# RWKV chunk: both heads' inverse products as one product, the outputs of a unit at its end

## The chip, the core and the metric

One core of a Trainium2 chip runs the kernel in one launch. The metric is the device time of one execution in microseconds, as the median of several runs. The engines are named as in the profile: PE is TensorE's matmul, PEld its weight load, DVE is VectorE, ACT is ScalarE, POOL is GpSimd and SP is SyncE, which issues the DMAs.

## The reference

One layer of a decoder for 1024 prompt tokens and 8 sample tokens. It projects the normalised input, runs an RWKV-7 recurrence (8 heads of 64) beside a diagonal state-space branch, merges the two through gates, and ends with a convolutional feed-forward net, a per-layer embedding and a norm. The change lies in the recurrence, which is, for one head:

```
sa  = S @ (-kk_t)
S   = S * w_t + sa (kk_t * a_t)^T + v_t k_t^T
y_t = S @ r_t
```

The results are all outputs y, the last states and the projected rows, in fp32.

## The kernel before

All arithmetic of TensorE is fp32 or a pair of float32r parts. A float32 product is issued by the program once and stands in the trace as two passes, each with its own weight load.

**Stream.** Most of the time goes to large projections (tile psm, `mtile` and `mt`): weights come by DMA (wraw), are split in two float32r parts (whi on ACT, wlo on POOL or DVE), and three products per 128x128 weight tile go into one of three PSUM banks (pool pm). In the stretch of interest these are the last gate tiles (344 columns, inputs h1h, h1l), then the GLU of the state-space branch (zh, zl), then the first half of the merge and feed-forward part for 512 tokens (mid, act).

**Units.** The recurrence is worked in 8 units (`build_rwkv`, line 1626 on): a unit is a pair of heads p (two heads of 64 lie on the 128 partitions) and a half hf of the prompt, 512 tokens, that is NC = 8 chunks of CH = 64 tokens. `prepare` makes a unit's inputs (`stage_a`, elementwise; `stage_g`, the products within chunks and the inverse of their triangular part), `chain` walks the 8 chunks, and `post` norms the outputs and sends them to DRAM. `prepare(n + 1)` is recorded ahead of `chain(n)`.

**Within chunks.** `stage_g` (line 1424) multiplies BK and AR of each chunk and head, masks the 128x128 result into Gm (DVE, four chunks at once), and transposes BK into BT. Gm holds for each chunk and head 128 columns: 64 for the inverse (A part) and 64 for the outputs (r part). The lower half of the A columns is replaced by its product with v (tile gvp, ACT). The inverse of the unit triangular 64x64 blocks is made in 32x32 blocks: two DMAs through DRAM, 31 steps on DVE (Tm), two DMAs back, and 2 x 16 products of 32x32 (mgp). Gm, BT and UV have two buffers, so the preparation of a unit can write them when the chain two units earlier has ended.

**Chain.** For chunk c (line 1520 on), with the state S of both heads as a block diagonal 128x128 tile: (1) pp = AR^T S, one 128x128 product; (2) DVE adds Gm's upper A rows into pe; (3) up, the inverse product: for each head a product with 64 output rows, Gm's 64 A columns as weights and 64 columns of pe moving, both into partitions 0 to 63 of up; (4) the outputs of the chunk before (`inner`): for each head, UV as weights and Gm's 64 r columns moving, into partitions 64h to 64h + 63 of the bank Y; (5) DVE copies up into UV; (6) su = BT^T UV, a 128x128 product; (7) Y += S^T r, a 128x128 product against 64 columns; (8) for each head DVE makes the new S from su and the decayed old one (sw, ACT). pp, up and su are three 128-column parts of one PSUM bank (tile chp); Y fills another bank (tile Yps), of which there is one. The products of (3) and (4) have the shape 128x64 in the profile, all others of the chain 128x128. The first chunk of a unit has no `inner`; the outputs of its last chunk stand after the loop.

**Order.** No engine's order is written out by hand: `Sched` records each operation with its dependencies, an estimated cost and a priority, and issues the operations engine by engine in the order of modelled time (`run`, line 354, `issue`, line 378; every issued instruction therefore stands on line 417). A lower number goes first: weight loads and the emptying of the stream's banks have HI, units have SIDE + 100000 n + 20000 k (k = 0 preparation, 1 chain, 2 post), the stream has MAIN. So a stream product is taken when no operation of a unit is ready by the planner's clock. A change of TensorE's shape is planned at 90 ns (SWITCH). `then` adds a dependency for the plan alone, so that a product isn't taken before some other operation.

Of the kernel before, what the change touches and what calls it, by code (L numbers as in the profile page):

```python
# [9 lines left out]
F32 = mybir.dt.float32  # L10
F32R = mybir.dt.float32r
AF = mybir.ActivationFunctionType
# [3 lines left out]
MUL, ADD, SUB, MAX, MIN = ALU.mult, ALU.add, ALU.subtract, ALU.max, ALU.min  # L16

P = 128
# [9 lines left out]
CH = 64  # L28
HW = 512
NC = HW // CH  # L30
# [1257 lines left out]
def build_rwkv(g, rp, pb, pch, py, I, O, Pd, Wd, Ad, Yd, sg, ssh, omu, pc, pcs, dscr, dap, dma,  # L1288
               epst, rsqrt):
    V, S, G, T, _ = g.engines()  # L1290
# [9 lines left out]
    mask4 = cc("mask")[:, None, :].to_broadcast([P, 4, 128])  # L1300
# [40 lines left out]
    for k in range(2):  # L1341
        t = rp.tile([P, P], F32, name=f"pe{k}")
# [80 lines left out]

    def stage_g(p, hf, a):
        AR, BK, v = a["AR"], a["BK"], a["v"]
        Gm = rp.tile([P, NC, 2, P], F32, name="Gm", tag="Gm", bufs=2)
        BT = rp.tile([P, NC, P], F32, name="BT", tag="BT", bufs=2)
        UV = rp.tile([P, NC, P], F32, name="UV", tag="UV", bufs=2)
        fl = lambda z: z.rearrange("p a b -> p (a b)")
        free = [G.memset(z, 0.0) for z in (Gm[:, 0, 0, 0:1], BT[:, 0, 0:1], UV[64:128, 0, 0:1])]  # L1430
        mm = lambda i, *a: g.rec("PE", "matmul", T.ns.matmul, a, dict(start=True, stop=True),
                                 (free[i],))
        tr = lambda i, *a: g.rec("PE", "transpose", T.ns.transpose, a, {}, (free[i],))
        for c4 in range(0, NC, 4):
            gp = [big(f"gp{h}").rearrange("p (c t) -> p c t", t=P) for h in range(2)]
            for j in range(4):
                for h in range(2):
                    hs = slice(64 * h, 64 * h + 64)
                    mm(0, gp[h][:, j], fl(BK[hs, c4 + j]), fl(AR[hs, c4 + j]))
            for h in range(2):  # L1440
                V.tensor_tensor(Gm[:, c4:c4 + 4, h], gp[h], mask4, op=MUL)
            tp = big("tpp").rearrange("p (c t) -> p c t", t=P)
            for j in range(4):
                tr(1, tp[:, j], fl(BK[:, c4 + j]), ident)
            S.activation(BT[:, c4:c4 + 4], tp, AF.Copy)
            vp = big("vpp").rearrange("p (c t) -> p c t", t=P)
            for c in range(c4, c4 + 4):
                if c == 0:
                    mm(2, vp[64:128, 0], v[:, 0:CH], ident)
                else:  # L1450
                    tr(2, vp[:, c - c4], v[:, (c - 1) * CH:(c + 1) * CH], ident)
            S.activation(UV[64:128, c4:c4 + 4], vp[64:128], AF.Copy)

        for c4 in range(0, NC, 4):
            vp = big("gvp")[64:128].rearrange("p (c h t) -> p c h t", h=2, t=64)
            for c in range(c4, c4 + 4):
                for h in range(2):
                    T.matmul(vp[:, c - c4, h], Gm[64:128, c, h, 0:64],
                             UV[64:128, c, 64 * h:64 * h + 64], start=True, stop=True)
            S.activation(Gm[64:128, c4:c4 + 4, :, 0:64], vp, AF.Copy)  # L1460


        gs = Gm.rearrange("p a b t -> p (a b) t")
        dg = [gs[32 * k:32 * k + 32, :, 32 * k:32 * k + 32] for k in range(2)]
        ld = dscr_ring("ld")
        for k in range(2):
            dma(dap(ld, 16384 * k, [[32, 32], [1024, 2 * NC], [1, 32]]), dg[k])
        Tm = rp.tile([P, 8, 32], F32, name="Tm", tag="Tm", bufs=2)
        tmp = rp.tile([P, 8, 32], F32, name="Tt", tag="Tq", bufs=2)
        dma(Tm, I["con"][:, nc_:nc_ + 256].rearrange("p (a b) -> p a b", b=32))  # L1470
        L = rp.tile([P, 31, 32], F32, name="Lj", tag="Lj", bufs=1)
        for r in range(4):
            dma(L[32 * r:32 * r + 32], dap(ld, 0, [[1024, 32], [1, 31 * 32]]))
        for j in range(31):
            n, w = j // 4 + 1, 31 - j
            if n == 1:
                V.scalar_tensor_tensor(Tm[:, 0, j + 1:], L[:, j, j + 1:], Tm[:, 0, j:j + 1],
                                       Tm[:, 0, j + 1:], op0=MUL, op1=ADD)
                continue
            V.tensor_tensor(tmp[:, :n, :w], L[:, None, j, j + 1:].to_broadcast([P, n, w]),  # L1480
                            Tm[:, :n, j:j + 1].to_broadcast([P, n, w]), op=MUL)
            V.tensor_tensor(Tm[:, :n, j + 1:], Tm[:, :n, j + 1:], tmp[:, :n, :w], op=ADD)
        xd = dscr_ring("xd")
        dma(dap(xd, 0, [[32, P], [4096, 8], [1, 32]]), Tm)
        for k in range(2):
            dma(dg[k], dap(xd, 512 * k, [[1024, 32], [32, 2 * NC], [1, 32]]))

        av = rp.tile([64, 2 * NC, 32], F32, name="av", tag="av", bufs=1)
        V.transpose(av[0:32], dg[0])
        mp = big("mgp").rearrange("p (a t) -> p a t", t=32)  # L1490
        for j in range(2 * NC):
            T.matmul(mp[32:64, j], gs[0:32, j, 32:64], av[0:32, j], start=True, stop=True)
        S.activation(av[32:64], mp[32:64], AF.Copy)
        mp = big("mgp").rearrange("p (a t) -> p a t", t=32)
        for j in range(2 * NC):
            T.matmul(mp[0:32, j], av[32:64, j], gs[32:64, j, 32:64], start=True, stop=True)
        S.activation(gs[0:32, :, 32:64], mp[0:32], AF.Copy)
        return dict(Gm=Gm, BT=BT, UV=UV)
# [7 lines left out]
    def chain(p, hf, a, b):  # L1506
        AR, WC, Gm, BT, UV = a["AR"], a["WC"], b["Gm"], b["BT"], b["UV"]
        Y = py.tile([P, NC, CH], F32, name="Yps", tag="Y")
        ch = pch.tile([P, 3, P], F32, name="chp", tag="ch")
        pp, up, su = ch[:, 0], ch[0:64, 1], ch[:, 2]  # L1510
        heads = [slice(64 * h, 64 * h + 64) for h in range(2)]

        def then(op, *a, **k):
            g.rec("PE", "matmul", T.ns.matmul, a, k, (op,))

        def inner(c, op, first):
            for h, hs in enumerate(heads):
                then(op, Y[hs, c], UV[:, c, hs], Gm[:, c, h, 64:128], start=first, stop=True)

        for c in range(NC):  # L1520
            n = hf * NC + c
            So, Sn = St[p, n % 2], St[p, (n + 1) % 2]
            first = n == 0

            if not first:
                T.matmul(pp, AR[:, c].rearrange("p a b -> p (a b)"), So, start=True, stop=True)
            pe = rhs[n % 2]
            gv = Gm[64:128, c, :, 0:64]  # L1530
            if first:
                got = V.tensor_copy(pe[0:64].rearrange("p (h t) -> p h t", t=64), gv)
            else:
                h2 = lambda z: z.rearrange("p (h t) -> p h t", t=64)
                got = V.tensor_tensor(h2(pe[0:64]), h2(pp[0:64]), gv, op=ADD)
            for h, hs in enumerate(heads):
                T.matmul(up[:, hs], Gm[:, c, h, 0:64], pe[:, hs], start=h == 0, stop=h == 1)
            if c:
                inner(c - 1, got, n == 1)
            got = V.tensor_copy(UV[0:64, c], up)  # L1540
            sw = rp.tile([P, P], F32, name="sw", tag="sw", bufs=2)
            for hs in heads:
                if not first:
                    S.activation(sw[hs, hs], So[hs, hs], AF.Copy, scale=WC[hs, c:c + 1])
            T.matmul(su, BT[:, c], UV[:, c], start=True, stop=True)
            if not first:
                then(got, Y[:, c], So, AR[:, c, 1], start=True, stop=False)
            for hs in heads:
                if first:
                    done = V.tensor_scalar(Sn[hs, hs], su[hs, hs], WC[hs, c:c + 1], None, op0=MUL)  # L1550
                else:
                    done = V.scalar_tensor_tensor(Sn[hs, hs], su[hs, hs], WC[hs, c:c + 1],
                                                  sw[hs, hs], op0=MUL, op1=ADD)
            if n == 2 * NC - 1:
                for hs in heads:
                    dma(O["wkv_p"][p][hs], Sn[hs, hs])
        inner(NC - 1, done, False)
        Y = Y.rearrange("p c t -> p (c t)")
        hi = rp.tile([P, HW], F32R, name="yh", tag="ysq", bufs=1)
        lo = claimed("yl", F32R)  # L1560
        S.activation(hi, Y, AF.Copy)
        V.tensor_tensor(lo, Y, hi.bitcast(F32), op=SUB)
        return hi, lo
# [204 lines left out]
```

## Time and profile before

| | us |
|---|---|
| median of 3 runs | 1861.35 |
| lowest, highest | 1857.27, 1863.98 |
| the profiled execution | 1858.5 |
| its span | 1856.7 |
| first to last inverse product (chp<-pe) | 335.4 to 827.2 |

The page gives each engine's busy time in the span. In the timeline of TensorE a row has its start, its length, the tile written and those read, the shape of the weights and of the moving data, and how many passes it merges. Lengths of matmuls are modelled and overlap, so the distance between two starts is the time that TensorE gave to the first. The clock that the throttle granted is a share of full speed.

### The profile page before, as it was taken

How to read it: one execution, taken by the hardware profiler on the slowest of the kernel's cores; microseconds unless marked ns; L12 is line 12 of the kernel's file. 1: busy time of each engine (PE TensorE's matmuls, PEld its weight loads, DVE VectorE, ACT ScalarE, POOL GpSimd, SP SyncE). 2: the span in 40 equal slices, each digit the busy share in tenths (PEclk: the TensorE clock that was granted, in tenths of full speed). 3: DMA queues.
4: the chain of work that ended last, by engine and by line, in shares of the span. 5: the costliest groups of instructions: out<-in, count | busy, mean ns of one | idle time of the engine just before them, and what ended most of it. 6: DMA issues, size and time to landing. Idle time of an engine off the chain costs nothing.

```text
span 1856.7 us, 32382 instructions
## 1 busy us (share of the span) xinstructions
PE 1799.0 (97%) x11946; PEld 1616.2 (87%) x11946; DVE 1135.5 (61%) x2376; ACT 810.6 (44%) x1445; POOL 738.7 (40%) x1071
## 2 busy tenths in 40 slices
PE   7999999999999999999999999999999999999997
PEld 6988888888889988987788888888888999999997
DVE  8899357758776568767655334335646445445475
ACT  4242443355544555554533333334655333323364
POOL 0000022233332444236654545455656444444464
PEclk9998998989999999999999999999999999999999
DMA  5534864313322264345633323223233333233332
GB/s 199 160 112 151 261 212 121 102 55 97 114 72 82 92 192 133 106 145 173 215 127 114 97 91 94 92 93 103 91 99 98 106 92 95 89 92 98 87 94 89
DMA packets 157949, 219.80 MB, mean 118 GB/s; under 512 B 48208, under 2 KB 81488, under 8 KB 157648
## 3 DMA queue, kind: packets, MB, share of 16 engines
q1 hardware_dynamic: 157792, 217.74, 37.7%
q8 instruction: 94, 1.54, 0.4%
q14 instruction: 63, 0.52, 0.1%
HBM read 174.94 MB, written 42.92 MB: 117 GB/s over the span
## 4 chain that ended last, share of the span: by engine, by line
PE 71%; DVE 10%; DMA 4%; ACT 3%; issue 3%; POOL 2%; SPq 1%; POOLq 0%; DVEq 0%; ACTq 0%
PE psm L417 62%; PE chp L417 2%; PE gp L417 1%; DMA yf<-yq 1%; DVE Tm L417 1%; PE gvp L417 1%; DVE Tt L417 1%; PE Yps L417 1%; DMA raw<-pd 1%; SPq L417 1%; DVE m L417 1%; DVE cv L417 1%; POOL wlo L417 1%; DMA wraw<-in_w_rw_out 1%; DVE Xi L417 1%
## 5 line engine op out<-in xcount | busy, mean ns | idle before, releaser
L417 POOL TENSOR_TENSOR wlo<-wraw,whi 128x512 fp32r<-128x512 f32 (+2 forms) x432 | 546.3, 1271 | 455.1 <-ACT whi L417 424.1
L417 PE MATMUL psm<-act,whi 128*128 128x260 f32 (+1 forms) x2880 | 651.9, 320 | 2.2 <-ACT whi L417 1.6
L417 PEld LDWEIGHTS psm<-act,whi 128*128 128x128 f32 x2880 | 479.8, 188 | 49.3 <-ACT whi L417 2.6
L417 ACT ACTIVATE whi<-wraw 128x512 fp32r<-128x512 f32 (+2 forms) x468 | 276.9, 597 | 447.9 <-PE psm L417 280.0
L417 PE MATMUL psm<-act,wlo 128*128 128x260 f32 (+1 forms) x1440 | 459.5, 322 | 0.0
L417 PE MATMUL psm<-mid,whi 128*128 128x260 f32 (+1 forms) x1344 | 306.1, 321 | 3.3 <-DVE cv L417 2.3
L417 PEld LDWEIGHTS psm<-act,wlo 128*128 128x128 f32 x1440 | 270.2, 188 | 23.5 <-issue 0.5
L417 PE MATMUL psm<-h1h,whi 128*128 128x344 f32 x816 | 271.0, 333 | 11.6 <-DVE h1h L417 11.3
L417 PE MATMUL psm<-h1h,wlo 128*128 128x344 f32 x816 | 270.7, 332 | 0.3 <-DVE wlo L417 0.2
L417 PE MATMUL psm<-h1l,whi 128*128 128x344 f32 x816 | 270.7, 332 | 0.1
L417 PEld LDWEIGHTS psm<-mid,whi 128*128 128x128 f32 x1344 | 222.7, 189 | 21.9 <-DVE cv L417 2.5
L417 PE MATMUL psm<-mid,wlo 128*128 128x260 f32 (+1 forms) x672 | 213.7, 322 | 0.0
L417 PEld LDWEIGHTS psm<-h1h,whi 128*128 128x128 f32 x816 | 156.7, 192 | 15.2 <-ACT h1h L417 11.3
L417 DVE TENSOR_TENSOR x<-psm,x 128x260 f32<-128x260 f32 (+1 forms) x160 | 84.6, 532 | 132.7 <-PE psm L417 132.6
L417 PEld LDWEIGHTS psm<-h1l,whi 128*128 128x128 f32 x816 | 157.0, 192 | 3.6 <-issue 0.9
L417 PEld LDWEIGHTS psm<-h1h,wlo 128*128 128x128 f32 x816 | 156.7, 192 | 3.7 <-DVE wlo L417 0.9
L417 PEld LDWEIGHTS psm<-mid,wlo 128*128 128x128 f32 x672 | 126.5, 189 | 9.6 <-POOL wlo L417 0.6
L417 DVE TENSOR_TENSOR ta<-psm,rs 128x260 f32<-128x260 f32 (+1 forms) x66 | 34.0, 516 | 139.0 <-PE psm L417 132.1
L417 DVE SCALAR_TENSOR_TENSOR cv<-ta,par,cv 128x512 f32<-128x512 f32 x88 | 89.7, 1019 | 38.3 <-ACT cv L417 36.9
L417 DVE TENSOR_TENSOR mid<-cv,mid 128x260 fp32r<-128x260 f32 (+1 forms) x84 | 67.3, 808 | 34.0 <-ACT mid L417 33.9
L417 ACT ACTIVATE sw<-S,WC 64x64 f32<-64x64 f32 x120 | 41.4, 345 | 74.5 <-DVE S L417 69.7
L417 ACT ACTIVATE cv<-cv 128x512 f32<-128x512 f32 (+1 forms) x44 | 28.0, 636 | 87.6 <-DVE cv L417 87.6
(348 smaller groups left out, 2557.3 us busy)
## 6 DMA issues: line engine op xcount, KB each, us to landing
wraw<-in_w_ffn_in SPq DMA_DIRECT2D x176, 256.0 KB, 2.7
wraw<-in_w_in SPq DMA_DIRECT2D x68, 256.0 KB, 3.4
wraw<-in_w_ffn_out SPq DMA_DIRECT2D x64, 192.0 KB, 2.4
gd<-gt SPq DMA_DIRECT2D x16, 516.0 KB, 3.2
wraw<-in_w_out SPq DMA_DIRECT2D x32, 256.0 KB, 2.9
wraw<-in_w_ple_gate SPq DMA_DIRECT2D x32, 256.0 KB, 2.7
wraw<-in_w_ffn_out SPq DMA_DIRECT2D x32, 256.0 KB, 3.2
pd<-pt SPq DMA_DIRECT2D x12, 516.0 KB, 3.8
```

What stands on the lines that cost most here:

```text
L417: o.fn(*o.args, **o.kw)
```

## The change

`Gm` gets its A and r parts as the outer of its column dimensions, so that the 64 A columns of both heads of a chunk lie side by side as 128. The inverse product becomes one 128x128 product against all 128 columns of pe; its result has both heads' blocks on the diagonal (partitions 0 to 63 with columns 0 to 63, partitions 64 to 127 with columns 64 to 127) and two cross blocks that nobody reads. DVE copies the two diagonal blocks in two instructions, the second from partitions 64 to 127 to partitions 0 to 63. `inner` is gone from the loop: after the last chunk, 16 products (8 chunks, 2 heads) add the outputs to Y, planned after the last state update. Only the first product into Y starts the bank; all others add or write where nothing stands yet.

```diff
@@ stage_g
-        Gm = rp.tile([P, NC, 2, P], F32, name="Gm", tag="Gm", bufs=2)
+        Gm = rp.tile([P, 2, NC, 2, CH], F32, name="Gm", tag="Gm", bufs=2)
+        halves = lambda z: z.rearrange("p c (k t) -> p k c t", t=CH)
...
-                V.tensor_tensor(Gm[:, c4:c4 + 4, h], gp[h], mask4, op=MUL)
+                V.tensor_tensor(Gm[:, :, c4:c4 + 4, h], halves(gp[h]), halves(mask4), op=MUL)
...
-                    T.matmul(vp[:, c - c4, h], Gm[64:128, c, h, 0:64],
+                    T.matmul(vp[:, c - c4, h], Gm[64:128, 0, c, h],
...
-            S.activation(Gm[64:128, c4:c4 + 4, :, 0:64], vp, AF.Copy)
+            S.activation(Gm[64:128, 0, c4:c4 + 4], vp, AF.Copy)
-        gs = Gm.rearrange("p a b t -> p (a b) t")
+        gs = Gm[:, 0].rearrange("p a b t -> p (a b) t")
@@ chain
-        pp, up, su = ch[:, 0], ch[0:64, 1], ch[:, 2]
+        pp, up, su = ch[:, 0], ch[:, 1], ch[:, 2]
-        def inner(c, op, first):
-            for h, hs in enumerate(heads):
-                then(op, Y[hs, c], UV[:, c, hs], Gm[:, c, h, 64:128], start=first, stop=True)
...
-            for h, hs in enumerate(heads):
-                T.matmul(up[:, hs], Gm[:, c, h, 0:64], pe[:, hs], start=h == 0, stop=h == 1)
-            if c:
-                inner(c - 1, got, n == 1)
-            got = V.tensor_copy(UV[0:64, c], up)
+            T.matmul(up, Gm[:, 0, c].rearrange("p h t -> p (h t)"), pe, start=True, stop=True)
+            got = V.tensor_copy(UV[0:64, c, 0:64], up[0:64, 0:64])
+            V.tensor_copy(UV[0:64, c, 64:128], up[64:128, 64:128])
...
-                then(got, Y[:, c], So, AR[:, c, 1], start=True, stop=False)
+                then(got, Y[:, c], So, AR[:, c, 1], start=c == (hf == 0), stop=False)
...
-        inner(NC - 1, done, False)
+        for c in range(NC):
+            for h, hs in enumerate(heads):
+                then(done, Y[hs, c], UV[:, c, hs], Gm[:, 1, c, h], start=False,
+                     stop=c == NC - 1)
```

## Rows read from the trace of the kernel before

**Rows 1.** the page, part 1: TensorE's busy time, share of the span, instructions.

```profile
PE 1799.0 (97%) x11946; PEld 1616.2 (87%) x11946; DVE 1135.5 (61%) x2376; ACT 810.6 (44%) x1445; POOL 738.7 (40%) x1071
```

**Rows 2.** windows, 335 to 831: us, busy us by engine (count), clock, DMA.

```profile
335.00:831.00 496.00, 482.24 (x3678) 427.39 (x3676) 353.17 (x954) 256.55 (x471) 168.59 (x300) 0.98 0.35 106
```

**Rows 3.** waits of TensorE, 335 to 831: total us, times, longest.

```profile
PE chp L417 <- DVE S L417: 2.8, 2, 2.2
...
PE chp L417 <- DVE UV L417: 1.7, 2, 0.9
```

**Rows 4.** timeline of TensorE, inverse products with outputs: start, length, tiles, shape, passes.

```profile
613.40 0.31 PE L417 MATMUL psm<-h1h,whi 128*128 128x344 f32 x1
613.65 0.39 PE L417 MATMUL chp<-pe,Gm 128*64 128x64 f32 x3
...
613.92 0.28 PE L417 MATMUL Yps<-Gm,UV 128*64 128x64 f32 x3
...
614.40 0.32 PE L417 MATMUL psm<-h1h,wlo 128*128 128x344 f32 x1
614.56 0.32 PE L417 MATMUL psm<-h1h,whi 128*128 128x344 f32 x1
```

**Rows 5.** timeline of TensorE, a dense 128x128 product of the chain.

```profile
612.38 0.32 PE L417 MATMUL psm<-h1l,whi 128*128 128x344 f32 x1
612.54 0.39 PE L417 MATMUL chp<-S,AR 128*128 128x128 f32 x2
...
612.93 0.32 PE L417 MATMUL psm<-h1h,whi 128*128 128x344 f32 x1
```

**Rows 6.** timeline of TensorE, inverse products of a unit's first chunk, no outputs.

```profile
721.25 0.32 PE L417 MATMUL psm<-zh,whi 128*128 128x344 f32 x1
721.79 0.45 PE L417 MATMUL chp<-pe,Gm 128*64 128x64 f32 x4 [0.22 <-ACT Gm L417]
...
722.43 0.32 PE L417 MATMUL psm<-zh,wlo 128*128 128x344 f32 x1
```

**Rows 7.** timeline of TensorE, the two outputs of a unit's last chunk alone.

```profile
418.30 0.32 PE L417 MATMUL psm<-h1h,wlo 128*128 128x344 f32 x1
418.55 0.34 PE L417 MATMUL Yps<-Gm,UV 128*64 128x64 f32 x4
...
419.08 0.32 PE L417 MATMUL psm<-h1l,whi 128*128 128x344 f32 x1
```

**Rows 8.** tile chp: operation, count, min/median/max ns, first and last start.

```profile
L417 PE MATMUL chp<-pe,Gm x256: 222/222/369, 335.4 to 827.2; 128*64 128x64 f32 x128
...
L417 DVE COPY UV<-chp x64: 272/277/284, 335.9 to 828.7; 64x128 f32<-64x128 f32 x64
```

**Rows 9.** timeline of VectorE: two 64x64 reads of chp.

```profile
615.21 0.60 DVE L417 SCALAR_TENSOR_TENSOR S<-chp,WC,sw 64x64 f32<-64x64 f32 x2
```

**Rows 10.** timeline of TensorE, the first product of the next stage's stream.

```profile
822.72 0.73 PE L417 MATMUL psm<-mid,whi 128*128 128x512 f32 x2
```

**Rows 11.** tile Gm: the product with the mask, columns as in rows 8.

```profile
L417 DVE TENSOR_TENSOR Gm<-gp,con x32: 640/681/694, 280.5 to 743.2; 128x512 f32<-128x512 f32 x32
```

**Rows 12.** tile ut: a read of PSUM that reorders its columns.

```profile
L417 DVE TENSOR_TENSOR ut<-psm,rstd x20: 147/747/783, 35.3 to 73.9; 128x344 f32<-128x344 f32 x8, 128x8 f32<-128x8 f32 x8, 128x336 f32<-128x336 f32 x4
```

**Rows 13.** the stretches at the lower clock: columns as in rows 2.

```profile
285.50:295.70 10.20, 10.20 (x56) 8.93 (x55) 5.33 (x6) 6.82 (x13) 4.70 (x5) 0.50 0.38 100
377.70:391.30 13.60, 13.60 (x74) 10.40 (x71) 4.32 (x9) 6.38 (x10) 3.91 (x4) 0.50 0.07 26
681.40:688.30 6.90, 6.48 (x21) 6.07 (x22) 6.24 (x24) 3.79 (x6) 2.01 (x4) 0.51 0.91 351
```

**Rows 14.** timeline of TensorE, two stream products at the lower clock.

```profile
285.70 0.49 PE L417 MATMUL psm<-h1l,whi 128*128 128x344 f32 x1
285.99 0.49 PE L417 MATMUL psm<-h1h,wlo 128*128 128x344 f32 x1
```

**Rows 15.** view of tile BT, who waited for it: us, times.

```profile
  POOL BT L417: 22.0, 5
```

More of the change, by code (lines that the diff above doesn't have):

```diff
@@ L1429, in stage_g @@
         fl = lambda z: z.rearrange("p a b -> p (a b)")
-        free = [G.memset(z, 0.0) for z in (Gm[:, 0, 0, 0:1], BT[:, 0, 0:1], UV[64:128, 0, 0:1])]
+        halves = lambda z: z.rearrange("p c (k t) -> p k c t", t=CH)
+        free = [G.memset(z, 0.0) for z in (Gm[:, 0, 0, 0, 0:1], BT[:, 0, 0:1], UV[64:128, 0, 0:1])]
         mm = lambda i, *a: g.rec("PE", "matmul", T.ns.matmul, a, dict(start=True, stop=True),
@@ L1529, in chain @@
             pe = rhs[n % 2]
-            gv = Gm[64:128, c, :, 0:64]
+            gv = Gm[64:128, 0, c]
             if first:
-                got = V.tensor_copy(pe[0:64].rearrange("p (h t) -> p h t", t=64), gv)
+                V.tensor_copy(pe[0:64].rearrange("p (h t) -> p h t", t=64), gv)
             else:
                 h2 = lambda z: z.rearrange("p (h t) -> p h t", t=64)
-                got = V.tensor_tensor(h2(pe[0:64]), h2(pp[0:64]), gv, op=ADD)
-            for h, hs in enumerate(heads):
-                T.matmul(up[:, hs], Gm[:, c, h, 0:64], pe[:, hs], start=h == 0, stop=h == 1)
-            if c:
-                inner(c - 1, got, n == 1)
-            got = V.tensor_copy(UV[0:64, c], up)
+                V.tensor_tensor(h2(pe[0:64]), h2(pp[0:64]), gv, op=ADD)
+            T.matmul(up, Gm[:, 0, c].rearrange("p h t -> p (h t)"), pe, start=True, stop=True)
+            got = V.tensor_copy(UV[0:64, c, 0:64], up[0:64, 0:64])
+            V.tensor_copy(UV[0:64, c, 64:128], up[64:128, 64:128])
             sw = rp.tile([P, P], F32, name="sw", tag="sw", bufs=2)
```

## The prediction

> **What bounds the kernel now.** I read the page's busy shares first, then the windows over the stretch in which the eight units run, then TensorE's waits, then its timeline instruction by instruction. TensorE is busy for 97% of the span [rows 1], and in the 496 us of the units it is busy for 482 us, with VectorE at 353 and ScalarE at 257 [rows 2]. The units' chain alone could not fill it: what fills it is the stream of large products (tile psm), which the planner lets in whenever the chain has nothing ready. The chain is the smaller partner, and TensorE waits for it almost never: 2.8 us for the state update and 1.7 us for the copy of the inverse product, in the whole stretch [rows 3]. So a microsecond of TensorE's time that the chain no longer takes is taken by the stream, and the end moves by it. What the change is worth must be read from start to start on TensorE's timeline: the modelled lengths there overlap.
>
> **The inverse product and its outputs.** A stream product starts 0.16 us after the one before it (614.40 to 614.56 [rows 4]); two such steps are 0.32. Where a chunk's four passes of the inverse product and four passes of the previous chunk's outputs stand between two stream products, three stream products span 613.40 to 614.40, 1.00 us: the chain took 0.68 [rows 4]. A dense product of the chain, 128 wide and two passes long, spans 612.38 to 612.93, 0.55 us: it took 0.23 [rows 5]. The new inverse product has exactly that shape (128x128 against 128 columns), so I take this row for it. Each chunk that has both today loses 1.00 - 0.55 = 0.45 us. There are 8 units of 8 chunks; in 7 of each the outputs ride along, so 56 x 0.45 = 25.2 us go.
>
> The first chunk of a unit has the inverse product alone: 721.25 to 722.43, 1.18 us. Its start is late (0.54 after the stream product, where rows 4 show 0.25), since it waited for ScalarE; without that 0.29 it is 0.89. It loses 0.89 - 0.55 = 0.34; 8 x 0.34 = 2.7 us go [rows 5, 6]. The outputs of a unit's last chunk stand alone at its end: 418.30 to 419.08, 0.78 us, less two stream steps 0.46 us [rows 7]; 8 x 0.46 = 3.7 us go.
>
> **The outputs made together.** In their place comes, once in a unit, a block of 16 products in the 64-wide shape, 32 passes. What is a pass more worth? Four passes of the inverse product last 0.45, three 0.39: 0.06 a pass when all go to one half of the output partitions [rows 4, 6]. Four passes of outputs, two for each head, last only 0.34 [rows 7]: the two heads' halves run side by side, so that two passes cost one step. The new block has 28 passes more than the one in rows 7: side by side 14 x 0.06 = 0.84, one after the other 28 x 0.06 = 1.68. I take side by side, since these are the same instructions in the same order of heads. A unit's block then takes 0.46 + 0.84 = 1.30 us, eight of them 10.4; at the other end 17.1.
>
> **Where the saving comes from, and a rule against it.** The outputs of rows 7 take 0.46 us for two steps of 0.06: some 0.34 is the way into the 64-wide shape and out of it. Today it is paid once a chunk, and the change pays it once a unit. The row above says this: dense 0.23, against 0.46 for four narrow passes that even run side by side [rows 5, 7]. The Trainium skill (TensorEngine Tiling (Array Packing), Overview, Theoretical Speedup) has the opposite advice for operands up to 64 wide: split the array, up to twice the speed; a dense product of two heads computes two cross blocks that nobody reads. The trace agrees with it on the packing itself and not on this use. The same page's Key Properties say that a change of the tiling mode drains the engine, without a figure; the figure here is the 0.34.
>
> **What is added elsewhere.** The copy of the inverse product is two copies of 64x64 in place of one of 64x128 (0.28 us [rows 8]). Two 64x64 reads of the same tile last 0.60 together [rows 9], so at most 0.32 more a chunk; at the least nothing. VectorE's 64 x 0.32 = 20 us more fit into the 143 us that it idles in the stretch [rows 2]. On the chain it is partly paid back: from the stream product before it to its end the inverse product takes 0.25 + 0.45 = 0.70 now [rows 4, 6], and 0.16 + 0.39 = 0.55 dense [rows 5]. So a chunk's chain grows by at most 0.17 us, 11 us over 64 chunks, all of it covered by stream products; the last of them before the next stage is followed at 822.72 by that stage's own stream [rows 10], so the cover lasts to the end of unit 7. Without the cover it would cost those 11 us.
>
> The mask product writes the same 512 columns in another order, 681 ns now, 32 times [rows 11]. The nearest row of a read that reorders is ut, 747 ns for about 344 columns, or 2.2 ns a column against 1.3 [rows 12]: bounds 0 (as many columns, so no gain) and 0.45 us each, 14 us of VectorE in all, ahead of a unit and hidden by the stream. I take 0, since runs of 64 columns stay together. The two DMA legs of the inverse move the same runs of 32 numbers from another stride, as many issues as before: nothing, on any queue. The outputs' block waits for the last state update by plan and for data long there; behind it on TensorE stands stream work, which it delays by its own length, already counted. The output bank is emptied about 1 us later, and the next stage's stream begins in the middle of unit 7 [rows 10], so nobody idles for it.
>
> **The sum.** Gone 25.2 + 2.7 + 3.7 = 31.6, come 10.4: 21.2 us less. The profiled execution takes 1858.5 us (span 1856.7 and 1.8 around it), 2.9 below the median of the runs, 1861.35. So 1837 by its own time and 1840 as a median. Both ends: outputs one after the other cost 6.7 more; and where a chunk's products stand next to other narrow work of the next unit, the way in and out stays. If 20 of the 56 stood so, 20 x 0.34 = 6.8 would stay. With both, 7.7 us are saved and the time is 1854.
>
> **Rivals.** (a) The clock. TensorE runs at the lower of its two levels (0.50, that is 1.2 of 2.4 GHz) in three stretches of the units, 30.7 us in all [rows 13]; there a stream product takes 0.29, not 0.16 [rows 14], so each us at that level gives away 0.45. If the change frees all three, 13.8 us more go: 1826. If it brings another of 13.6 us, 6.1 come back: 1846. For it: the three follow side work and gaps, and that work moves. Against it: rows show the engine busy throughout two of them, so what sets it off isn't plain. The Trainium skill (TensorE: Matmul & The Clock Gate, Part 1) says that the low clock is the default and activity lifts it; denser products would then help if anything, and no row here shows it.
>
> (b) The saving is thinner: outputs one after the other and switches that stay, as in the sum's other end, 1847 to 1854. For it: preparation of the next unit runs in narrow shapes beside every chain.
>
> (c) Nothing changes: the way in and out is hidden, or packing alone counts. By passes, today's 56 x 6 x 0.06 + 8 x (4 + 2) x 0.06 = 23 us, the new 64 x 0.23 + 8 x 0.96 = 22: 1860. By the skill's packing rule alone it would come out here. Against it: rows 5 and 7 price the way directly. The case that the planner breaks the outputs' block up with stream products, so that the changes of shape stay, ends here too.
>
> (d) Slower: the chain becomes the bound. Each preparation of a unit waits for the end of the chain two units earlier, 22.0 us in five waits [rows 15], and that chain grows by up to 8 x 0.17 + 1.3 = 2.7 us. From the point at which the stream runs dry before unit 7 ends, this is paid in full and the saving is idle time: 8 x 2.7 = 22 us, 1861 + 22 = 1883. Against it: TensorE waits 4.5 us for the chain today [rows 3], and the next stage's stream starts before unit 7 ends [rows 10].
>
> **Chances.** Forecast (saving 14 to 22 us, 1839 to 1847) 0.60; clock for the better (1826 to 1838) 0.13; thinner (1847 to 1855) 0.14; nothing 0.07; slower 0.06. A measurement of this kernel tells 0.3%, 5.6 us, from no change. Faster by more: 0.60 + 0.13 + 0.14 = 0.87, of which I give 0.02 to the edge at 1856: 0.85. Same 0.09, slower 0.06. The range 1826 to 1856 leaves out (c), (d) and the edge, some 0.15, and a little below.
>
> **What would show it.** Right: the inverse product as two passes in the 128x128 shape, three stream products around it 0.55 us apart; 16 outputs in a row once a unit, lasting about 1.1 to 1.2 us; about 21 us less to the start of the last stage, and the work after the units as long as before. Wrong: outputs broken up by stream products, a block of 2 us, TensorE's waits for the chain growing from 4.5 us to more than 15, or other stretches at the lower clock.

## The result, and the profile after

The changed kernel takes 1842.89 us (median of 4 runs, 1840.03 to 1844.13), the kernel before 1859.85 beside it (4 runs, 1857.27 to 1863.98): ratio 0.990, 95% interval 0.986 to 0.994. The forecast was 1840, the range 1826 to 1856. The profiled execution takes 1844.13 us, its span 1842.1. The total came out as forecast; the way to it did so only in part, and the experiments are about that part.

First the page's busy shares, the row that answers to [rows 1].

```profile
PE 1782.6 (97%) x11818; PEld 1610.1 (87%) x11818; DVE 1152.1 (63%) x2440; ACT 803.8 (44%) x1441; POOL 740.9 (40%) x1071
```

TensorE has 128 passes less (four narrow ones became two, 64 times) and is as full as before. VectorE has 64 instructions more, the second copies. Next the tiles chp and Gm, as in [rows 8] and [rows 11].

```profile
L417 PE MATMUL chp<-pe,Gm x128: 270/275/422, 332.8 to 846.2; 128*128 128x128 f32 x128
...
L417 DVE COPY UV<-chp x128: 203/222/227, 333.2 to 846.8; 64x64 f32<-64x64 f32 x128
```

The inverse product has the dense shape. Its last one stands at 846.2 in place of 827.2: the chains end later. From the first to the last inverse product they take 513.4 us, before 491.8. The product with the mask takes 684 ns (32 of them), against 681.

Now TensorE's timeline, columns as in [rows 4]: a dense inverse product, then a second one.

```profile
627.25 0.31 PE L417 MATMUL psm<-h1h,wlo 128*128 128x344 f32 x1
627.40 0.38 PE L417 MATMUL chp<-pe,Gm 128*128 128x128 f32 x2
627.54 0.41 PE L417 MATMUL psm<-h1h,whi 128*128 128x344 f32 x1
627.79 0.32 PE L417 MATMUL psm<-h1l,whi 128*128 128x344 f32 x1
...
584.67 0.32 PE L417 MATMUL psm<-h1l,whi 128*128 128x344 f32 x1
584.83 0.47 PE L417 MATMUL chp<-pe,Gm 128*128 128x128 f32 x2
585.05 0.41 PE L417 MATMUL psm<-h1h,wlo 128*128 128x344 f32 x1
585.29 0.32 PE L417 MATMUL psm<-h1h,whi 128*128 128x344 f32 x1
```

From the stream product ahead to the second one behind, the first spans 0.54 us, as the row it was priced from [rows 5], the second 0.62. The difference lies between the two passes (0.38 and 0.47 long together). It goes with the data of the product, pe, which VectorE makes just ahead of it; first the row for the product at 627.40, then that for 584.83:

```profile
626.82 0.28 DVE L417 TENSOR_TENSOR pe<-chp,Gm 64x128 f32<-64x128 f32 x1 [1.04 <-PE chp L417]
...
584.47 0.28 DVE L417 TENSOR_TENSOR pe<-chp,Gm 64x128 f32<-64x128 f32 x1
```

pe is ready 0.30 us before the first product starts and 0.08 us before the second. 43 dense products stand with nothing but stream products around them. 22 of them start 0.20 us or more after pe is ready: their passes start 0.11 apart. 15 start 0.054 to 0.056 after it, sooner than which none starts: their passes start 0.21 apart, and from their start to the second stream product behind they take 0.485 in place of 0.38. The narrow product of the kernel before doesn't show this: 6 of its 38 start as early, and take 0.75 as the others do. The outputs at a unit's end:

```profile
478.51 0.32 PE L417 MATMUL psm<-h1h,wlo 128*128 128x344 f32 x1
478.76 1.15 PE L417 MATMUL Yps<-Gm,UV 128*64 128x64 f32 x32
479.84 0.42 PE L417 MATMUL psm<-h1h,whi 128*128 128x344 f32 x1
480.10 0.32 PE L417 MATMUL psm<-h1l,whi 128*128 128x344 f32 x1
```

In all eight units the 32 passes stand in one piece and last 1.15 us; here 478.51 to 480.10 less two stream steps is 1.28, where the forecast had 1.30.

What TensorE waits for from 335 to 850 us, columns as in [rows 3]:

```profile
PE mps L417 <- DVE yl L417: 4.8, 4, 1.7
PE chp L417 <- DVE S L417: 2.7, 2, 1.7
...
PE chp L417 <- DVE UV L417: 1.2, 2, 0.9
...
PE chp L417 <- DVE pe L417: 1.0, 1, 1.0
```

The chain is waited for as little as before (4.9 us, before 4.5 [rows 3]). The first row is new. It is the norm of a unit's outputs, which reads the bank that now fills last. Other waits are gone, so that all waits of TensorE in this stretch together are 15.9 us, before 13.7. ScalarE's, VectorE's and TensorE's timelines at one such place:

```profile
418.62 0.60 ACT L417 ACTIVATE yh<-Yps 128x512 fp32r<-128x512 f32 x1
```

```profile
419.49 0.22 DVE L417 TENSOR_TENSOR Tt<-Lj,Tm 128x64 f32<-128x64 f32 x1
419.74 0.22 DVE L417 TENSOR_TENSOR Tm<-Tm,Tt 128x64 f32<-128x64 f32 x1
...
421.07 0.23 DVE L417 TENSOR_TENSOR Tt<-Lj,Tm 128x65 f32<-128x65 f32 x1
421.22 0.69 DVE L417 TENSOR_TENSOR yl<-Yps,yh 128x512 fp32r<-128x512 f32 x1
```

```profile
421.96 0.51 PE L417 MATMUL mps<-yl,bor 128*128 128x512 f32 x1 [1.31 <-DVE yl L417]
```

yh is done at 419.22, yet yl starts at 421.22: the plan has put seven instructions of the next unit's inverse between them on VectorE, and TensorE's queue has the product that reads yl next, with the stream behind it.

Last the stretches of the units at the lower clock, columns as in [rows 13].

```profile
262.90:266.30 3.40, 2.91 (x10) 2.81 (x11) 1.64 (x2) 2.96 (x4) 2.38 (x4) 0.50 0.94 282
375.60:385.80 10.20, 10.20 (x84) 8.73 (x82) 1.50 (x4) 4.88 (x7) 1.36 (x2) 0.50 0.13 49
672.50:679.30 6.80, 6.60 (x31) 6.30 (x32) 1.28 (x4) 3.93 (x6) 1.31 (x2) 0.50 0.59 169
```

They are 20.4 us in place of 30.7 [rows 13]. If the n-th stream product of one trace is set against the n-th of the other, the changed kernel is 13.2 us ahead at the 3500th, behind the last unit in both, 14.7 at the 8000th and 14.8 at the 9400th: nearly all of the gain is made while the units run, and nothing is given back after.

### The profile page after: what moved, and what is told of

It reads as the page before. It is cut to its first block, busy times and chain, and to the rows that moved or that the text cites. A ratio compares the mean times of both kernels' runs of the same rounds, so it can differ in the third digit from the quotient of the medians.

```text
span 1842.1 us, 32187 instructions
## 1 busy us (share of the span) xinstructions
PE 1782.6 (97%) x11818; PEld 1610.1 (87%) x11818; DVE 1152.1 (63%) x2440; ACT 803.8 (44%) x1441; POOL 740.9 (40%) x1071
## 4 chain that ended last, share of the span: by engine, by line
PE 49%; DVE 2%; ACT 1%; POOL 0%; issue 0%; DMA 0%; SPq 0%; POOLq 0%; ACTq 0%; DVEq 0%
PE psm L417 49%; DVE x L417 1%; DVE cv L417 1%; DVE act L417 1%; DMA wraw<-in_w_rw_out 0%; POOL wlo L417 0%; PE pstt L417 0%; DVE mid L417 0%; POOL x L417 0%; SPq L417 0%; DVE tg L417 0%; PE m L417 0%; ACT whi L417 0%; ACT cv L417 0%; ACT L417 0%
## 5 line engine op out<-in xcount | busy, mean ns | idle before, releaser
L417 POOL TENSOR_TENSOR wlo<-wraw,whi 128x512 fp32r<-128x512 f32 (+2 forms) x432 | 552.4, 1285 | 477.9 <-ACT whi L417 444.5
L417 PE MATMUL psm<-h1h,whi 128*128 128x344 f32 x816 | 270.7, 333 | 11.3 <-DVE h1h L417 11.1
L417 DVE TENSOR_TENSOR mid<-cv,mid 128x260 fp32r<-128x260 f32 (+1 forms) x84 | 69.2, 831 | 22.5 <-ACT mid L417 21.7
L417 PE MATMUL psm<-zh,whi 128*128 128x344 f32 x192 | 62.9, 328 | 2.4 <-DVE gt L417 2.4
```

Source lines behind the costliest of these rows:

```text
L417: o.fn(*o.args, **o.kw)
```

## How the runs are compared: the time at full clock

The mean granted clock differs from run to run of one and the same kernel, and the time follows it. Two runs of the kernel before: clock 0.987, 1850.63 us; clock 0.979, 1862.17 us. With a granted clock of c, a share 2(1 - c) of the span lies at the lower level, and each us there gives away 0.45 (0.29 against 0.16 for a stream product [rows 14]). So I bring each run to full clock as its time x (1 - 0.9 x (1 - c)). For 29 runs of the kernel before this gives a median of 1829.0 with a standard deviation of 2.5 us, and 1829.2 and 1828.8 on the two other chips. The clock column is the mean over a kernel's runs.

| kernel | median us | ratio to before, 95% | clock | at full clock |
|---|---|---|---|---|
| before (three chips) | 1861.9, 1861.3, 1865.5 | | 0.981, 0.980, 0.979 | 1829 |
| e0_after (the change again) | 1841.72 | 0.990, 0.986 to 0.994 | 0.987 | 1820 |
| e1_dense_alone | 1865.02 | 1.001, 0.998 to 1.004 | 0.986 | 1841 |
| e2_end_alone | 1863.40 | 1.002, 0.999 to 1.005 | 0.982 | 1834 |
| e3_halves | 1861.37 | 1.001, 0.998 to 1.005 | 0.983 | 1833 |
| e4_slack | 1845.00 | 0.990, 0.986 to 0.993 | 0.980 | 1811 |
| e5_act_copy | 1855.32 | 0.996, 0.993 to 0.999 | 0.984 | 1828 |
| e6_third_copy | 1846.82 | 0.993, 0.990 to 0.997 | 0.984 | 1824 |
| e7_before_slack | 1839.63 | 0.987, 0.982 to 0.992 | 0.985 | 1814 |
| e8_halves_slack | 1849.70 | 0.992, 0.989 to 0.995 | 0.988 | 1829 |
| e9_slack_300 | 1846.96 | 0.991, 0.988 to 0.994 | 0.984 | 1821 |
| e10_slack_700 | 1834.06 | 0.987, 0.982 to 0.991 | 0.985 | 1814 |
| e11_end_slack | 1843.97 | 0.989, 0.986 to 0.991 | 0.985 | 1818 |

Of the 20 us between before and after, 9 are there at full clock. The other 11 are a higher granted clock: 0.9 x 1842 x (0.9872 - 0.9806) = 11. This split is an estimate: fitted to the runs of the kernel before, a clock lower by 0.01 costs 14, 19 and 16 us on the three chips, where the formula has 17. A difference of 2 or 3 us between two rows of the last column is hardly more than the spread of their runs.

## The experiments

None of them leaves out a part of the reference. The edits are against the changed kernel, that of e7 against the kernel before. "Block" below is the time that TensorE gives to a group of chain products between two stream products, from the stream product ahead to the second one behind, less 0.31 for two stream steps; medians over all blocks that stand alone. "Counted whole" is the sum of all blocks from 270 to 870 us that hold an inverse or output product, with whatever else stands in them, at full clock: 97.4 us before, 84.7 in the changed kernel, 85.2 in its repetition e0.

**e0: the change again, on the chip of e1 to e3.** Nothing is edited.

> The changed kernel again, on the same chip as the three beside it. Both theories: 15 to 17 us faster than the kernel before (ratio 0.991), with the narrow products gone from the loop.

1841.72: the result repeats.

**e1: the dense product alone**, the outputs back in the loop.

```diff
+        def inner(c, op, first):
+            for h, hs in enumerate(heads):
+                then(op, Y[hs, c], UV[:, c, hs], Gm[:, 1, c, h], start=first, stop=True)
...
+            if c:
+                inner(c - 1, got, n == 1)
...
-        for c in range(NC):
-            for h, hs in enumerate(heads):
-                then(done, Y[hs, c], UV[:, c, hs], Gm[:, 1, c, h], start=False,
-                     stop=c == NC - 1)
+        inner(NC - 1, done, False)
```

> The dense inverse product and its two copies, but the outputs of the chunk before back in the loop. Theory (what is paid for is the way into the 64-wide shape and out of it, 0.34 us): a chunk still goes there once, for the outputs: 64 x (0.23 + 0.46) = 44 us against 47 us before, so 3 us faster at most, ratio 0.998 to 1.000. Rival 1 (the dense product itself is the gain, two passes for four): most of the 17 us come, ratio under 0.995. Rival 2 (the second copy lies on the path): 5 to 11 us slower than before.

No gain. TensorE's timeline shows why:

```profile
621.78 0.32 PE L417 MATMUL psm<-h1h,whi 128*128 128x344 f32 x1
621.94 0.38 PE L417 MATMUL chp<-pe,Gm 128*128 128x128 f32 x2
622.25 0.34 PE L417 MATMUL Yps<-Gm,UV 128*64 128x64 f32 x4
622.52 0.42 PE L417 MATMUL psm<-h1l,whi 128*128 128x344 f32 x1
622.78 0.32 PE L417 MATMUL psm<-h1h,wlo 128*128 128x344 f32 x1
```

Three stream products span 1.00 us, as in the kernel before [rows 4]. The dense product goes in cheaply (0.16), but the way from it to the outputs takes 0.31 for two passes, and the first stream product behind takes 0.26, not 0.16. The median block is 0.77 against 0.69 before. At full clock e1 is even 12 us behind the kernel before, a little more than rival 2 gave. But the blocks counted whole are 12.6 us more than before, so the loss stands on TensorE at these products; in 13 of the 38 blocks that stand alone the dense product starts as soon as its data is there, as in the second example above. What part the second copy has in that was not tested in this kernel.

**e2: the outputs at the end alone**, the inverse product as before.

```diff
-        pp, up, su = ch[:, 0], ch[:, 1], ch[:, 2]
+        pp, up, su = ch[:, 0], ch[0:64, 1], ch[:, 2]
...
-            T.matmul(up, Gm[:, 0, c].rearrange("p h t -> p (h t)"), pe, start=True, stop=True)
-            got = V.tensor_copy(UV[0:64, c, 0:64], up[0:64, 0:64])
-            V.tensor_copy(UV[0:64, c, 64:128], up[64:128, 64:128])
+            for h, hs in enumerate(heads):
+                T.matmul(up[:, hs], Gm[:, 0, c, h], pe[:, hs], start=h == 0, stop=h == 1)
+            got = V.tensor_copy(UV[0:64, c], up)
```

> The outputs of a unit made together at its end, but the inverse product as two narrow products into the same 64 partitions with one copy, as before. Theory: a chunk still goes into the 64-wide shape once, for the inverse: 64 x 0.57 + 8 x 1.28 = 47 us against 47 us, so no change, ratio 0.998 to 1.002. Rival (keeping the outputs out of the loop is the gain, the dense product adds little): ratio 0.995 or less.

No gain either. The block has lost the outputs and is still 0.57 (before 0.69): from a stream product into the narrow shape it is still 0.26, and the first stream product behind still takes 0.26, both 0.16 between stream products; this stays, 64 times.

```profile
509.73 0.32 PE L417 MATMUL psm<-h1h,whi 128*128 128x344 f32 x1
509.99 0.45 PE L417 MATMUL chp<-pe,Gm 128*64 128x64 f32 x4
510.36 0.42 PE L417 MATMUL psm<-h1l,whi 128*128 128x344 f32 x1
510.62 0.32 PE L417 MATMUL psm<-h1h,wlo 128*128 128x344 f32 x1
```

**e3: the changed kernel with the inverse product in two halves**, each head's into its own 64 partitions; copies and outputs as after the change, so only the shape of one product differs.

```diff
-            T.matmul(up, Gm[:, 0, c].rearrange("p h t -> p (h t)"), pe, start=True, stop=True)
+            for h, hs in enumerate(heads):
+                T.matmul(up[hs, hs], Gm[:, 0, c, h], pe[:, hs], start=True, stop=True)
```

> As the changed kernel, but the inverse product as two narrow products into the two halves of the partitions, so that they can run side by side as the two heads' outputs do; copies and outputs as changed. Theory (change of shape counts): 0.34 + 0.12 = 0.46 a chunk against 0.23 dense, 64 x 0.23 = 15 us slower than the changed kernel, about 2 us faster than before. Rival (packing counts, the change of shape is hidden): 0.12 against 0.23, 7 us faster than the changed kernel.

```profile
583.78 0.32 PE L417 MATMUL psm<-h1h,wlo 128*128 128x344 f32 x1
584.03 0.34 PE L417 MATMUL chp<-pe,Gm 128*64 128x64 f32 x4
584.30 0.43 PE L417 MATMUL psm<-h1h,whi 128*128 128x344 f32 x1
584.56 0.32 PE L417 MATMUL psm<-h1l,whi 128*128 128x344 f32 x1
```

The four passes now last 0.34 in place of 0.45, side by side, and the block is 0.47; the dense one in the changed kernel is 0.31. That is 0.16 x 64 = 10 us by blocks, and 13 at full clock (1833 against 1820). The whole gain is gone, as the theory of the shape has it: 0.47 a block against its 0.46. The Trainium skill (TensorEngine Tiling (Array Packing), Key Properties) says that changing the mode drains the engine; the trace fits that, with 0.25 from a stream product to the first narrow one against 0.16 to a dense one, but doesn't show the drain itself.

**e4: more allowance.** The planner adds 200 ns to every dependency from another engine to TensorE. The idea of the run: with more, it takes chain products later, and fewer find their data late.

```diff
-    LATE = {"PE": 200, "DVE": 35, "ACT": 35, "POOL": 70, "SP": 60}
+    LATE = {"PE": 450, "DVE": 35, "ACT": 35, "POOL": 70, "SP": 60}
```

> The changed kernel, with the planner's allowance between another engine's result and the TensorE product that needs it raised from 200 to 450 ns. Theory (the changed kernel lost some 5 us to TensorE's waits for the emptying of the output bank and some 4 us to dense products that came before their data, because the unplanned cost of the changes of shape was slack that is now gone): the waits for yl fall from 4.8 to under 2.5 us, fewer dense products have their passes 0.2 us apart, and the time falls by 3 to 8 us against the changed kernel, ratio to before 0.986 to 0.988. Rival (those waits replace stream time that would have been lost anyway, or later products cost as much): as the changed kernel, 0.990.

At full clock 9 us better (1811 against 1820), in time nothing (1845 against 1842): its clock is 0.980. The expected reason didn't come. The waits for yl fall to 3.2 us, not under 2.5, all waits of TensorE from 335 to 850 us grow from 15.9 to 18.8, and 14 of 46 dense products that stand alone start as soon as their data is there, against 15 of 43. What is less is the blocks counted whole, 75.1 us against 84.7, and the side work that stands alone between stream products, 88.8 against 94.1. Its profile has five stretches at the lower level in the units, 47.7 us:

```profile
sum 47.70, PE 47.70 PEld 39.53 DVE 17.85 ACT 20.24 POOL 11.45; mean PE 9.54 PEld 7.91 DVE 3.57 ACT 4.05 POOL 2.29
```

TensorE is busy in all of it, so the loss cannot be read from its busy share.

**e5 and e6: the second copy**, on ScalarE in e5, done twice on VectorE in e6.

```diff
-            V.tensor_copy(UV[0:64, c, 64:128], up[64:128, 64:128])
+            S.activation(UV[0:64, c, 64:128], up[64:128, 64:128], AF.Copy)   # e5
...
+            V.tensor_copy(UV[0:64, c, 64:128], up[64:128, 64:128])           # e6: once more
```

> The changed kernel, the second of the two copies on ScalarE instead of VectorE, so that both run at once. If the copies are hidden by the stream, as predicted: no change against the changed kernel, ratio to before 0.988 to 0.992. If the chain's length counts: 64 x 0.2 = 13 us faster than the changed kernel at the most, ratio 0.983.

> The changed kernel with the second copy done twice, one 64x64 copy of some 0.22 us more on VectorE and on the chain of each chunk. Hidden by the stream: ratio to before 0.989 to 0.992, no change. On the path: 64 x 0.2 = 13 us slower than the changed kernel, 0.997.

A third copy of 0.22 us a chunk is 14 us of VectorE; it costs 5 us as a median and 4 at full clock, so most of it is hidden, not all. On ScalarE the copy takes as long (0.221 against 0.210 us) and costs 13.6 us, 8 at full clock. By its blocks it is the state product behind the copy that is dearer: 0.59 against 0.46, so 5 us over the 40 that stand alone. Of the two places the change chose the cheaper one.

**e7: the kernel before with the allowance of e4.**

> The kernel before with the allowance of 450 ns. Theory: its plan already had slack, since the changes of shape cost 0.34 us where the plan has 0.18: no change, ratio 0.998 to 1.002. Rival (the allowance is a gain by itself, whatever the change): as much faster as the changed kernel with it, 0.996 to 0.998.

This is the run that upsets a simple story. Not one product is changed, and it gains 21.7 us, 15 at full clock: as much as the change, or more. At an allowance of 450 the change itself is worth 3 us at full clock (1814 against 1811), hardly more than the spread, and in time nothing (1839.63 against 1845.00).

**e8, e11: e3 and e2 with that allowance.** The edits are those of e3 and e2 with that of e4.

> The changed kernel with the inverse product as two 64-wide products (as in e3_halves) and with TensorE's allowance in the plan at 450 in place of 200 (as in e4_slack), so that waits made by the plan are out of both sides of the comparison with e4_slack. Theory (the change of shape has a price on TensorE itself): 64 ways into and out of the 64-wide shape remain, the end is 12 to 20 us later than e4_slack's 1845, so 1857 to 1865, ratio to the kernel before 0.997 to 1.002; at equal granted clock 1823 to 1826 against 1811. Rival (e3_halves lost its 20 us to waits that its plan made, not to the shape): with the allowance it is as fast as e4_slack, 1841 to 1849, ratio 0.988 to 0.993.

> The kernel with the outputs at a unit's end and the inverse product as two 64-wide products into the same 64 partitions (as in e2_end_alone), allowance 450. If neither half of the change gains alone because the way into the 64-wide shape is still paid 64 times: it stays behind e4_slack by 14 to 22 us, 1859 to 1867, at equal clock 1824 to 1833. If the half's gain was only hidden by waits that its plan made: 1840 to 1850, as the kernel before with the same allowance (1840).

e8's blocks are e3's (0.47), and at full clock it is 18 us behind e4: the theory. In time it is 5 behind, since its clock is 0.988: the rival by the median. e11 has e2's blocks (0.57, so 64 x 0.26 = 17 us over a dense one) and is only 7 behind e4 at full clock, 1 us ahead in time: the theory's 14 to 22 did not come, and the other forecast of 1840 to 1850 did. So the block prices hold in every trace, but a plan made with another allowance moves more than they do.

**e9, e10: other allowances, the change kept**, 300 and 700.

> The changed kernel with the allowance at 300. Theory (the waits for data that the plan lets in too early eat about half of the saving; the allowance gives them back, and the rest is granted clock): at equal clock between the changed kernel's 1820 and e4_slack's 1811, about 1815; as a median 1832 to 1845, by the clock of its runs. Rival (the allowance only shifts the plan by chance): at equal clock anywhere within 6 us of 1820, with no order among 200, 300 and 450.

> The changed kernel with the allowance at 700. Theory: the waits were already gone at 450, so TensorE gains nothing more, while each chunk's chain grows by some 0.25 us for each of its four handovers to TensorE, 64 us over 64 chunks, which the stream still covers: at equal clock 1809 to 1815, median 1838 to 1850. Rival (the chain becomes the bound once it is stretched): the stream runs dry before the last unit ends and TensorE idles, 1860 to 1890.

At full clock 1820, 1821, 1811, 1814 for 200, 300, 450, 700: no smooth curve, so the 1815 forecast for 300 was wrong. The dense blocks have no order either: medians of 0.31, 0.37, 0.30, 0.23, and 15 of 43, 21 of 39, 14 of 46, 8 of 46 products that start as soon as their data is there. Only at 700 are most of these gone, and the stretched chain isn't the bound.

```profile
571.03 0.32 PE L417 MATMUL psm<-h1h,wlo 128*128 128x344 f32 x1
571.19 0.38 PE L417 MATMUL chp<-pe,Gm 128*128 128x128 f32 x2
571.33 0.40 PE L417 MATMUL psm<-h1h,whi 128*128 128x344 f32 x1
571.57 0.32 PE L417 MATMUL psm<-h1l,whi 128*128 128x344 f32 x1
```

1834.06 is the best median of all, 0.9865 of the kernel before; e7, with 0.9871, can't be told from it.

## Why the prediction was right, and where it was not

**The price of the shape: right.** In the cleanest blocks the dense inverse product takes the 0.23 forecast and saves the 0.45 of the sum. e1, e2 and e3 show that it is the change of shape and not the passes: taking the outputs away, or packing the halves side by side, or making one of two products dense leaves it in place, and none gains. e8 against e4 shows it at another allowance, 18 us at full clock. Rival (c), that packing alone counts, falls with e3.

**The outputs' block: right** (1.28 against 1.30, side by side).

**The number of chunks that get the saving: mis-sized.** The term 56 x 0.45 = 25.2 takes each chunk at the cleanest price. Of the 43 dense blocks that stand alone the median is 0.31 and not 0.23, since many are let in just as their data comes and then take 0.10 more; against the 0.69 of before that saves 0.38. And 18 of the 64 chunks have their inverse product in a block with side work (24 before). Counted whole, the inverse and output blocks take 84.7 us in place of 97.4: 12.7 less where the sum had 21.2. The dense product of the chain that the change left alone (AR^T S) has become dearer too, 0.33 in place of 0.24 as a median, some 4 us over the 45 that stand alone; the sum had nothing for that. In size this is near rival (b), but of its two reasons one didn't come, the outputs do run side by side, and the late data isn't among them.

**"Nobody idles" for the later output bank: wrong.** It was costed at nothing, since the bank is emptied about 1 us later. But yl falls behind the next unit's inverse steps on VectorE, and TensorE waits 4.8 us for it. This was the wait to name: what the plan has queued on VectorE ahead of the step that was moved. As other waits went, all of them together grew by 2.2 us only.

**The copies: right in kind.** Two copies take 0.44 in place of 0.28 us; the forecast had up to 0.32 more. They are hidden for the most part: a third one costs 4 us of its 14 (e6). The mask's order costs 3 ns.

**The chain as bound, rival (d): it didn't come.** The wait of BT for the chain fell from 22.0 [rows 15] to 11.3 us, and an allowance of 700 (e10), which plans each handover of the chain to TensorE later, does no harm. But the chains did grow by 21.6 us from the first to the last inverse product, where the forecast had 11 at most; the stream covered it.

**The clock, rival (a): came in part.** The profile has 10 us less at the lower level, and over all runs the clock is 0.987 against 0.981, worth 11 us. Without it the result would have been about 1853, inside the range, near the thin end. So 1840 was met by a product saving of 9 us, thinner than forecast, and a clock gain, to which the prediction gave 0.13. That the two add up to the forecast is luck.

**What stays open.** Take the median blocks times their number, against before, and beside them the times at full clock: e1 +6 and +12, e2 0 and +5, e3 -7 and +4, the change -17 and -9. The order is that of the blocks, but all four times come out 5 to 11 us above them. Counted whole, with side work and late products, the blocks are at +12.6, +7.0, -1.7 and -12.7, within 6 us of the times. e7 is 15 us below with unchanged blocks, 2.0 us less counted whole. Its side work that stands alone takes 90.2 us in place of 97.2 and its waits from 335 to 850 us 8.9 in place of 13.7; the rest was not found. So part of what a run gains or loses lies beside the products that were edited, and no run changes the products while it keeps the plan. The kernel before was run at 450 only, not at 300 or 700. Nor was it settled why the plans differ in clock: e4 and e10 differ by one number and have 0.980 and 0.985.

## What to carry to other kernels

Price a narrow product on TensorE from the stream product ahead to the second one behind, and count its changes of shape: here every version that left a single narrow product in each step gained nothing at the first allowance (e1, e2, e3). Where a planner lays out the order, run the planner's own allowance on the old kernel as well before a gain of 1% is put down to the edit, since that alone was worth as much here. And before two kernels within 1% are compared, bring both to the same granted clock.

## What was not expected of the hardware

The granted clock of one kernel varies from run to run between 0.968 (1878.8 us) and 0.988 (1848.9 us) over the 67 runs of the kernel before, so 30 us for 0.02, more than the change is worth. A dense product of two passes that starts as soon as its data is there costs 0.10 us more behind its start (0.485 in place of 0.38): its passes start 0.21 us apart, not 0.11. In the changed kernel the second pass of all 21 such and nearly such products that stand alone starts 0.268 or 0.269 us after pe is ready, whenever the first one started. The narrow product shows no such price (0.75 either way). Why is not shown.
